# Side work of the SSD groups reordered in a hybrid GLA / Mamba-2 backbone: transposes on a second line, states in merged steps

## The chip, the core and the metric

The kernel runs on one core of a Trainium2 chip. Its engines are named as the profile names them: PE multiplies matrices (PEld loads its weights), DVE works on vectors, ACT evaluates functions and copies, POOL does further element-wise work, and SP issues the DMAs. Each engine executes its own instructions in the order in which the program lists them, and waits on semaphores where it needs another's result. The metric is the device time of one execution, in microseconds; a kernel is judged by the median of its runs.

## The reference

A backbone of two layers over 512 latent tokens and 256 context tokens, 1024 channels, all in float32. Layer 0 mixes tokens with chunked gated linear attention, layer 1 with a bidirectional Mamba-2 SSD; each mixer is followed by a squared-ReLU MLP of 4096 hidden channels, and every sub-layer is modulated and normalized. The change touches the SSD mixer alone. There a projection gives a gate z (2048 channels), x (2048), and for each of 8 groups a B and a C of 128 channels, and step sizes dt. x, B and C pass a centred convolution of five taps and a SiLU. A group has four heads of 64 channels. For each head and direction a state of 64 x 128 runs over the tokens:

```
cum = cumsum(dt * a)
decay = exp(cum[i] - cum[j]) for j <= i
y  = sum_j (C_i . B_j) * decay * dt_j * x_j   +   C_i . exp(cum_i) * s
s' = s * exp(last) + sum_j B_j * exp(last - cum_j) * dt_j * x_j
```

The context tokens are run first, forward and backward; their final states are the first states of the latent tokens. The output is (y_forward + y_backward + d * x) * SiLU(z), normalized, times an output matrix.

## The kernel before, in words

All large products are split: each float32 operand becomes a high and a low part (`wh`, `wl`, `xh`, `xl`), and a product is three matmuls (high-high, high-low, low-high; line 240). A weight tile of 128 x 1024 is loaded by SP into `raw` (four buffers), ACT casts the high part (L203), DVE subtracts for the low part (L204).

**Order.** The program lists the big projections in a row, and `worked` (line 179) counts their columns: each 768 columns are one step of a side clock. At each step the first generator of the list `side` may be advanced; it yields the number of steps that it wants to wait. So the work of group g, in `inner`, is dealt out between the projections of group g + 1. `drain` finishes a generator that is still there at a group's end. After that a scheduler lays down the order of each engine's instructions; it may move an instruction ahead where it believes the inputs ready.

**The SSD stage.** Tokens are in six chunks of 128: four latent (0 to 3), two of context (4, 5). For each of eight groups `group` projects and convolves B (`fB`), C (`fC`) and two tiles of x (`fx`), then projects two gate tiles (`gate_tiles`). A projection over both streams is 24 steps of the side clock, one over latent tokens alone 16, a group 120. A convolution (`conv`) is two ACT copies, one ACT and four DVE passes over 770 columns (L865, L867), then tanh and a last DVE pass, in two pieces for latent and context tokens (L869, L870).

Then `inner` does, in this order:

- `heads_rows`, `chunk_rows`: rows of cumulated decays are loaded from DRAM, broadcast to all partitions: `E` for whole heads, and per chunk two tiles `L`, one for each direction. There are seven `L` buffers. POOL masks each `L` (L912).
- `natural`: PE transposes `fB` and both `fx` chunk by chunk (L877); ACT copies the result to `Bn` and `xn` (L878; `xnat` in the profile).
- `prep`: DVE multiplies x of a chunk by its weights, in halves of 256 columns, one for each direction (L931, called by `scaled_by`). `dS`: PE multiplies by `Bn` (L943, L946).
- `chain`: one state step, a DVE product (L931) and a DVE sum (L951) of 256 columns. Eight of them, separately for the two directions, give the four states `ST` of each direction.
- the product of B and C of each chunk (`cb`, L963), copied to `cbs` by ACT (L965).
- `inter`: PE multiplies the states by `fC` (L986), DVE scales (L987, L989), POOL adds (L988).
- per chunk: `decays` (eight ACT exponentials of 128 columns, L998), `masks` (POOL adds both directions, L1001, which frees the second `L`; DVE multiplies by `cbs`, L1002), `outputs` (eight PE passes, L1009, and a DVE sum, L1012).
- the gated result `y` (L1031), its store, its square (ACT, L1036) and the sum of squares (POOL, L1037).

Small products share four PSUM banks (`sm`), the projections four others (`mm`). Behind the last group the output product starts with tiles loaded back and scaled (L1044, L1045).

## Time and profile before

| | |
|---|---|
| median of 3 runs | 1954.72 us (1950.36 to 1959.47) |
| profiled execution, span | 1959.6 us |
| PE busy | 1881.3 us (96%) |
| DVE, ACT, POOL busy | 1254.9, 798.6, 410.8 us |
| SSD groups | about 1015 to 1476 us of the span |
| one middle group | 60.5 us: PE 56.9, DVE 48.2, ACT 31.8, POOL 20.4 us |

The span is that of one execution, from the first to the last instruction; nothing of that execution is shown outside it. In the profile a row such as `PE sm L943 <- DVE xw L931: 14.6, 7, 3.6` says that PE, before writing a tile `sm` on line 943, waited for DVE's `xw` of line 931: 14.6 us in all, seven times, 3.6 us at most. A timeline row gives start, duration, engine, line, operation, out<-in, sizes, the number of instructions and, in brackets, the idle time before and who ended it. A matmul of float32 operands that are not split counts as two passes.

### The profile page before, as it was taken

Reading aid. Unit: us, or ns where it says so; the run is one execution under the profiler, and the core shown is the slowest. Engines: PE = TensorE matmul, PEld = TensorE weight load, DVE = VectorE, ACT = ScalarE, POOL = GpSimd, SP = SyncE. Lnnn points to the kernel's source line nnn. Section 1 sums busy time; section 2 is a strip of 40 time slices with the busy share of each in tenths; the row PEclk is TensorE's granted clock in tenths of the full one; section 3 lists DMA queues with packets and bytes.
Section 4 is the critical chain, followed back from the end, with each engine's and each line's share of the span. In section 5 each row is a group of like instructions: output and inputs, shape, how many; then the busy total and the mean of one; then the engine's idle time right before and its main releaser. Section 6 shows DMA issues by size and latency. Waiting matters only on the chain.

```text
span 1959.6 us, 29026 instructions
## 1 busy us (share of the span) xinstructions
PE 1881.3 (96%) x11405; PEld 1604.9 (82%) x11405; DVE 1254.9 (64%) x1929; ACT 798.6 (41%) x1386; POOL 410.8 (21%) x448
## 2 busy tenths in 40 slices
PE   7999999999999999999999999999999999999997
PEld 5988888788788888888897787777877788888886
DVE  4798887888655444324578888777887673333345
ACT  3445456454113123122366555455543353323231
POOL 2134242202002002010104432333321321102012
PEclk9999999999999999999999999999999999999999
DMA  8423313214444444313134433333434523333331
GB/s 329 156 73 114 104 36 106 65 55 150 141 142 140 138 137 135 116 41 116 33 107 121 129 115 112 104 101 129 121 100 132 164 73 105 96 99 96 96 89 54
DMA packets 78936, 219.01 MB, mean 112 GB/s; under 512 B 11056, under 2 KB 15792, under 8 KB 78800
## 3 DMA queue, kind: packets, MB, share of 16 engines
q1 hardware_dynamic: 78800, 217.17, 35.1%
q8 instruction: 89, 1.46, 0.3%
q14 instruction: 47, 0.39, 0.1%
HBM read 209.01 MB, written 8.13 MB: 111 GB/s over the span
## 4 chain that ended last, share of the span: by engine, by line
PE 63%; DVE 13%; DMA 7%; ACT 6%; POOL 5%; issue 5%; SPq 0%; DVEq 0%; POOLq 0%; ACTq 0%
PE mm L240 54%; DMA L<-crowc 4%; POOL L L1001 1%; ACT L L998 1%; DMA raw<-in_ada_wr_dram 1%; DVE A L593 1%; PE sm L943 1%; DVE raw L157 1%; DVE cv L867 1%; POOL L L912 1%; PE sm L676 1%; DVE wl L204 1%; POOL W L612 1%; PE sm L986 1%; PE mm L520 1%
## 5 line engine op out<-in xcount | busy, mean ns | idle before, releaser
L240 PE MATMUL mm<-xh,wh 128*128 128x512 f32 (+1 forms) x1824 | 554.2, 357 | 2.8 <-ACT xh L1044 2.6
L240 PE MATMUL mm<-xl,wh 128*128 128x512 f32 (+1 forms) x1824 | 550.0, 354 | 1.5 <-DVE xl L1045 1.5
L240 PE MATMUL mm<-xh,wl 128*128 128x512 f32 (+1 forms) x1824 | 549.7, 353 | 1.4 <-DVE wl L204 1.4
L203 ACT CAST wh<-raw 128x1024 fp32r<-128x1024 f32 (+3 forms) x227 | 227.8, 1004 | 658.5 <-PE mm L240 617.3
L204 DVE TENSOR_TENSOR wl<-raw,wh 128x1024 fp32r<-128x1024 f32 (+3 forms) x227 | 275.6, 1215 | 173.6 <-ACT wh L203 170.1
L240 PEld LDWEIGHTS mm<-xh,wh 128*128 128x128 f32 x1824 | 304.4, 189 | 54.4 <-ACT xh L1044 3.8
L240 PEld LDWEIGHTS mm<-xl,wh 128*128 128x128 f32 x1824 | 303.7, 189 | 50.6 <-issue 3.1
L240 PEld LDWEIGHTS mm<-xh,wl 128*128 128x128 f32 x1824 | 303.5, 189 | 50.7 <-DVE wl L204 2.5
L385 POOL TENSOR_TENSOR rq<-rr 128x768 f32<-128x768 f32 (+1 forms) x62 | 104.6, 1687 | 684.7 <-ACT rr L384 648.4
L240 PE MATMUL mm<-rl,wh 128*128 128x512 f32 x704 | 212.5, 355 | 3.8 <-DVE rl L387 3.8
L240 PE MATMUL mm<-rh,wl 128*128 128x512 f32 x704 | 212.4, 355 | 0.0
L240 PE MATMUL mm<-rh,wh 128*128 128x512 f32 x704 | 212.1, 355 | 0.0
L419 DVE SCALAR_TENSOR_TENSOR acc<-mm,row,acc 128x256 f32<-128x256 f32 (+1 forms) x182 | 100.7, 580 | 150.4 <-PE mm L240 150.0
L157 DVE SCALAR_TENSOR_TENSOR raw<-raw,srow 128x1024 f32<-128x1024 f32 x104 | 131.6, 1268 | 83.0 <-DMA raw<-in_ada_wr_dram 81.8
L867 DVE SCALAR_TENSOR_TENSOR cv<-pre,cvec,cv 128x770 f32<-128x770 f32 (+1 forms) x128 | 135.2, 1057 | 14.9 <-ACT cv L865 11.9
L240 PEld LDWEIGHTS mm<-rl,wh 128*128 128x128 f32 x704 | 116.0, 189 | 23.8 <-DVE rl L387 4.2
L240 PEld LDWEIGHTS mm<-rh,wh 128*128 128x128 f32 x704 | 116.1, 189 | 19.6
L240 PEld LDWEIGHTS mm<-rh,wl 128*128 128x128 f32 x704 | 116.1, 189 | 19.6
L998 ACT ACTIVATE L<-L,lcol 128x128 f32<-128x128 f32 x256 | 81.9, 393 | 69.1 <-POOL L L912 69.1
L387 DVE TENSOR_TENSOR rl<-rq,rh 128x768 fp32r<-128x768 f32 (+2 forms) x67 | 53.2, 794 | 64.0 <-POOL rq L385 63.7
L912 POOL TENSOR_SCALAR_AFFINE_SELECT L<-L 128x512 f32<-128x512 f32 x64 | 52.2, 817 | 142.5 <-DMA L<-crowc 141.4
L869 ACT ACTIVATE cf<-cv 128x512 f32<-128x512 f32 (+1 forms) x56 | 27.6, 533 | 86.5 <-DVE cv L867 86.5
(290 smaller groups left out, 2513.0 us busy)
## 6 DMA issues: line engine op xcount, KB each, us to landing
raw<-in_ffn_w_dram SPq DMA_DIRECT2D x112, 512.0 KB, 3.8
raw<-in_ada_wr_dram SPq DMA_DIRECT2D x80, 512.0 KB, 3.7
raw<-in_ssd_w_in_dram SPq DMA_DIRECT2D x48, 512.0 KB, 3.9
L<-crowc SPq DMA_DIRECT2D x64, 256.0 KB, 3.8
raw<-in_ada_w_dram SPq DMA_DIRECT2D x16, 512.0 KB, 9.1
raw<-in_gla_w_in_dram SPq DMA_DIRECT2D x16, 512.0 KB, 3.7
ec<-crow SPq DMA_DIRECT2D x64, 128.0 KB, 3.0
acc<-in_xT_dram SPq DMA_DIRECT2D x14, 384.0 KB, 6.9
```

The source lines that it names most:

```text
L157: nc.vector.scalar_tensor_tensor(o, raw, 1.0, srow[s], ALU.mult, ALU.mult, accum_out=t[:, b, s:s + 1])
L203: nc.scalar.copy(h, src)
L204: nc.vector.tensor_sub(l, src, h.bitcast(F32))
L240: nc.tensor.matmul(part_of(ps, t0, n), a[:, k, :], b[:, t0:t0 + n], start=(k == 0 and i == 0), stop=(k == kt - 1 and i == 2))
L385: eng.tensor_mul(q[:, a:b], r[:, a:b], r[:, a:b])
L387: nc.vector.tensor_sub(rl[:, a:b], q[:, a:b], rh[:, a:b].bitcast(F32))
L419: nc.vector.scalar_tensor_tensor(acc[m][:, t0:t0 + n], part_of(ps, t0, n), gate[:, m, s:s + 1], (src or acc)[m][:, t0:t0 + n], ALU.mult, A ...
L520: nc.tensor.matmul(ps[:, 256 * tt:256 * tt + 256], a, b, start=(k == 0 and i == 0), stop=(k == KT - 1 and i == 2))
L867: nc.vector.scalar_tensor_tensor(c[:, 0:n], pre[:, t:t + n], cw(t), c[:, 0:n], ALU.mult, ALU.add)
L869: nc.scalar.activation(f[:, t0:t1], c[:, t0 + d:t1 + d], AF.Tanh)
L912: nc.gpsimd.affine_select(out=L[z], in_=L[z], compare_op=ALU.is_ge, fill=NEG, base=0, pattern=[[0, 4], [1 - 2 * z, P]], channel_multiplier ...
L998: nc.scalar.activation(t[:, h, :], t[:, h, :], AF.Exp, bias=lcol[:, c, r:r + 1])
```

## The change

- **A second line of side work.** `worked` now advances two lists, `side` and `early`. A new generator `turned` is put on `early` as soon as both x tiles of a group are convolved, while its gate tiles are projected; it transposes B and the first x tile. The second x tile is transposed in `inner`, which stands on `side` as before. `Bn` and `xn` have two buffers each for that.
- **Context states summed in PSUM.** The weights `wc` of chunk 4 (forward) and 5 (backward) are multiplied once, in the set-up, by the decay over the other context chunk. The first state of both directions is then the sum of two products in one PSUM bank, which ACT copies.
- **Merged state chain.** The states are held as steps of both directions: `ST[i]` has the forward state of chunk i and the backward state of chunk 3 - i, with the decays of both in `dstep`. A step is a product and a sum of 512 columns; three steps make all states. `weighted` multiplies a chunk's x for both directions in one instruction; `ends` does chunks 0 and 3 in two halves.
- **Outputs in pairs.** Two chunks' products are written to one bank and added by one DVE sum of 512 columns.
- **Convolution.** Tanh and the last pass go over 770 columns at once; the context chunks are read two columns further on.
- `inner` yields other numbers, rows of chunk 0 and 1 are loaded at its start, chunks 2 and 3 after the second chunk's decays; `L` has eight buffers, `xt` four. The scratch that the program reserves for dynamic DMAs is set to 1024.

```diff
-LB = 7
-ZB = 2
-EB = 3
+LB = 8
+EB = 4
+NP = NT + 2
...
-    side, background = [], []
+    side, early, background = [], [], []
+    lanes = ((side, [0]), (early, [0]))
...
-            wait[0] -= 1
-            if wait[0] <= 0:
-                wait[0] = advance(side) or 1
+            for lane, wait in lanes:
+                wait[0] -= 1
+                if wait[0] <= 0:
+                    wait[0] = advance(lane) or 1
...
+            dtot = tt(sh, "dtot")
             nc.scalar.activation(dtot, po, AF.Exp)
+            for z, c in ((0, 4), (1, 5)):
+                zs = slice(32 * z, 32 * z + 32)
+                nc.vector.tensor_mul(wc[:, c, zs], wc[:, c, zs], dtot[:, 9 - c, zs])
+            nc.gpsimd.tensor_copy(dstep[:, :, 0, :], dtot[:, 0:3, 0:32])
+            for i in range(3):
+                nc.gpsimd.tensor_copy(dstep[:, i, 1, :], dtot[:, 3 - i, 32:64])
...
-            for t0, t1, d in ((0, 512, 0), (512, 768, 2)) if len(segs) > 1 else ((0, 512, 0),):
-                nc.scalar.activation(f[:, t0:t1], c[:, t0 + d:t1 + d], AF.Tanh)
-                nc.vector.scalar_tensor_tensor(f[:, t0:t1], f[:, t0:t1], 1.0, c[:, t0 + d:t1 + d], ALU.add, ALU.mult)
+            nc.scalar.activation(f[:, 0:n], c[:, 0:n], AF.Tanh)
+            nc.vector.scalar_tensor_tensor(f[:, 0:n], f[:, 0:n], 1.0, c[:, 0:n], ALU.add, ALU.mult)
...
             fx = [conv(2 * g + i, BOTH) for i in range(2)]
+            Bn = sp.tile([P, NCH, P], F32, tag="Bn", name=nm("Bn"), bufs=2)
+            xn = sp.tile([P, NCH, 256], F32, tag="xn", name=nm("xnat"), bufs=2)
+            early.append(turned(fB, fx, Bn, xn))
...
             drain()
-            side.append(inner(g, fB, fC, fx, zs))
+            drain(lane=early)
+            side.append(inner(g, fB, fC, fx, zs, Bn, xn))
+
+        def turned(fB, fx, Bn, xn):
+            yield 4
+            natural(fB, Bn)
+            yield 8
+            natural(fx[0], xn[:, :, 0:P])
+            yield 1
...
+            def weighted(c):
+                xw = sp.tile([P, 2, 256], F32, tag="xt", name=nm("xw"), bufs=EB)
+                w = wc[:, c, :].rearrange("p (z h) -> p z h", z=2)[:, :, heads]
+                x = xn[:, c, :].rearrange("p (h e) -> p h e", e=64).unsqueeze(1)
+                nc.vector.tensor_tensor(by_head(xw), x.to_broadcast(both), w.unsqueeze(3).to_broadcast(both), ALU.mult)
+                return xw
...
+            def step(i, d):
+                t = states()
+                w = dstep[:, i, :, heads].unsqueeze(3).to_broadcast(both)
+                nc.vector.tensor_tensor(by_head(t), by_head(ST[i]), w, ALU.mult)
+                nc.vector.tensor_add(t, t, d)
+                ST.append(t)
...
-            natural(fB, Bn)
-            yield 1
-            for i in range(2):
-                natural(fx[i], xn[:, :, i * P:(i + 1) * P])
-                yield 7
...
-            x4, x5 = prep((4, 4)), prep((5, 5))
-            yield 5
-            d4, d5 = dS(*x4), dS(*x5)
-            chain(ST[0][:, 0], d4[:, 0], 5, 0, d5[:, 0])
-            chain(ST[3][:, 1], d5[:, 1], 4, 1, d4[:, 1])
...
+            Rs, Ms = {0: chunk_rows(0), 1: chunk_rows(1)}, {}
+            x4, x5 = None, None
+            yield 2
+            natural(fx[1], xn[:, :, P:2 * P])
+            yield 2
+            x4, x5 = weighted(4), weighted(5)
+            xe = ends()
...
+            yield 8
+            x1 = weighted(1)
+            yield 3
+            d = sm_ps([P, 2, 256])
+            nc.tensor.matmul(d, Bn[:, 4, :], x4, start=True, stop=False)
+            nc.tensor.matmul(d, Bn[:, 5, :], x5, start=False, stop=True)
+            ST = [states()]
+            nc.scalar.copy(ST[0], d)
...
+            step(0, de)
+            yield 6
...
+            step(1, dd[0])
+            step(2, dd[1])
...
+            yield 4
+            decays(0)
+            yield 6
+            inter(0)
+            yield 5
+            inter(1)
+            yield 4
+            decays(1)
+            Rs[2] = chunk_rows(2)
+            Rs[3] = chunk_rows(3)
+            yield 14
+            outputs(0)
+            decays(2)
+            yield 14
+            decays(3)
+            yield 14
+            outputs(1)
+            yield 4
...
-    nc = _bacc.Bacc("TRN2", target_bir_lowering=False, num_devices=1)
+    nc = _bacc.Bacc("TRN2", target_bir_lowering=False, num_devices=1, dynamic_dma_scratch_size=1024)
```

The scheduler's order, not this text, decides what stands where. Ahead of the SSD stage and behind it the order of the kernel is the same. Three places in it, all at group 6; the numbers behind names are running ones, and differ between the two kernels.

ACT at the turn to the next group, before. `zs` are gate tiles, `Bn` and `xnat` the copies of transposes, `L` row tiles of the next group in their decays, `cbs` the copy of the product of B and C:

```order
L890 ACTIVATE zs_13147<-mm_13154 128x512
L203 CAST wh_13446<-raw_13444 128x1024
L878 COPY Bn_13211<-sm_13213 128x512
L878 COPY Bn_13211<-sm_13219 128x256
L878 COPY xnat_13212<-sm_13225 128x4x128
L878 COPY xnat_13212<-sm_13231 128x2x128
L998 ACTIVATE L_14084<-L_14084,lcol 128x128 x4
L878 COPY xnat_13212<-sm_13249 128x4x128
L878 COPY xnat_13212<-sm_13255 128x2x128
L998 ACTIVATE L_14136<-L_14136,lcol 128x128 x4
L965 COPY cbs_13309<-sm_13304 128x512
```

And now:

```order
L1014 ACTIVATE L_13742<-L_13742,lcol 128x128
L1014 ACTIVATE L_13929<-L_13929,lcol 128x128 x4
L203 CAST wh_13321<-raw_13319 128x1024
L898 ACTIVATE zs_13048<-mm_13055 128x512
L885 COPY xnat_12993<-sm_13126 128x4x128
L885 COPY xnat_12993<-sm_13132 128x2x128
L1014 ACTIVATE L_13930<-L_13930,lcol 128x128 x4
L974 COPY cbs_13152<-sm_13147 128x512
L1014 ACTIVATE L_13939<-L_13939,lcol 128x128 x4
L982 COPY ST_13181<-sm_13178 128x512
```

The copies of `Bn` and of the first x tile stand further ahead, out of these rows; the copies of the second x tile have one row tile's decays ahead of them, and behind them come two more, `L_13930` and `L_13939`, ahead of the copy of the first state.

POOL around the same place, now (`pre` are the margins of a convolution's input, `ssum` the sum of squares, AFFINE_SELECT the mask of a row tile, `TENSOR_TENSOR L` the sum of both directions, which frees the second tile's buffer):

```order
L1056 TENSOR_TENSOR ssum<-ssum,zs_12445 128x512
L1056 TENSOR_TENSOR ssum<-ssum,zs_12499 128x512
L926 AFFINE_SELECT L_13929<-L_13929 128x512
L862 MEMSET pre_13306 128x2
L863 MEMSET pre_13306 128x2
L1015 TENSOR_TENSOR L_13741<-L_13741,L_13742 128x512
L926 AFFINE_SELECT L_13930<-L_13930 128x512
L1015 TENSOR_TENSOR L_13929<-L_13929,L_13930 128x512
L926 AFFINE_SELECT L_13939<-L_13939 128x512
```

The buffer of `L_13742` goes to `L_13930`, and that of `L_13930` to `L_13939`, so each of these loads waits for the sum just above its mask; before, the same pairs of sum and mask stood there with the sums of squares between them.

DVE from the last gate tile on, now (`wl` a weight's low part, `xw` the weighted x, `L` the masked products, `ST` the states):

```order
L899 SCALAR_TENSOR_TENSOR zs_13048<-zs_13048,mm_13055 128x512
L940 TENSOR_TENSOR xw_13140<-xnat_12993,wc 128x512
L940 TENSOR_TENSOR xw_13142<-xnat_12993,wc 128x512
L948 TENSOR_TENSOR xw_13144<-xnat_12993,wc 128x256 x2
...
L1016 TENSOR_TENSOR L_13349<-L_13349,cbs_13152 128x512
L940 TENSOR_TENSOR xw_13183<-xnat_12993,wc 128x512
L957 TENSOR_TENSOR ST_13188<-ST_13181,dstep 128x512
L958 TENSOR_TENSOR ST_13188<-ST_13188,sm_13185 128x512
...
L957 TENSOR_TENSOR ST_13212<-ST_13209,dstep 128x512
L204 TENSOR_TENSOR wl_13443<-raw_13440,wh_13442 128x1024
L958 TENSOR_TENSOR ST_13212<-ST_13212,sm_13204 128x512
```

The masked products of all four chunks stand ahead of the first step; before, each stood behind some of the state steps, and the steps were sixteen instructions of 256 columns, those of the two directions in turn. A weight's low part stands between the product and the sum of the last step.

More of the change, by code (lines that the diff above doesn't have):

```diff
@@ L876, in natural @@
                 for c in range(c0, c1):
-                    nc.tensor.transpose(pt[:, c - c0, :], f[:, c * P:(c + 1) * P], ident)
+                    t0 = c * P + (2 if c >= NLC else 0)
+                    nc.tensor.transpose(pt[:, c - c0, :], f[:, t0:t0 + P], ident)
                 nc.scalar.copy(dst[:, c0:c1, :], pt[:, 0:c1 - c0, :])
@@ L913, in chunk_rows @@
                                             pattern=[[0, 4], [1 - 2 * z, P]], channel_multiplier=2 * z - 1)
-                    if z >= ZB:
-                        nc.gpsimd.tensor_add(L[z], L[z], hsl(lcol, c, z).unsqueeze(2).to_broadcast([P, 4, P]))
-                return L
-            Es = [heads_rows(i) for i in range(2)]
-            Bn = sp.tile([P, NCH, P], F32, tag="Bn", name=nm("Bn"), bufs=1)
-            xn = sp.tile([P, NCH, 256], F32, tag="xn", name=nm("xnat"), bufs=1)
-            natural(fB, Bn)
@@ L934, in prep @@
-            def prep(cs):
-                xw = sp.tile([P, 2, 256], F32, tag="xt", name=nm("xw"), bufs=EB)
-                for z, c in enumerate(cs):
-                    scaled_by(xw[:, z], xn[:, c], wc, c, z)
-                return xw, cs
-            def dS(xw, cs):
-                dp = sm_ps([P, 2, 256])
-                if cs[0] == cs[1]:
-                    nc.tensor.matmul(dp, Bn[:, cs[0], :], xw, start=True, stop=True)
-                else:
-                    for z, c in enumerate(cs):
-                        nc.tensor.matmul(dp[:, z], Bn[:, c, :], xw[:, z], start=True, stop=True)
-                return dp
@@ L949, in chain @@
-            def chain(dst, src, c, z, d):
-                scaled_by(dst, src, dtot, c, z)
-                nc.vector.tensor_add(dst, dst, d)
-            ST = [sp.tile([P, 2, 256], F32, tag="ST", name=nm("ST"), bufs=4) for _ in range(NLC)]
-            x4, x5 = prep((4, 4)), prep((5, 5))
-            yield 5
-            d4, d5 = dS(*x4), dS(*x5)
-            chain(ST[0][:, 0], d4[:, 0], 5, 0, d5[:, 0])
-            chain(ST[3][:, 1], d5[:, 1], 4, 1, d4[:, 1])
-            x03 = prep((0, 3))
+                return L
@@ new lines, in ends, with states @@
+            def ends():
+                xw = sp.tile([P, 2, 256], F32, tag="xt", name=nm("xw"), bufs=EB)
+                for z, c in enumerate((0, 3)):
+                    w = wc[:, c, 32 * z + 4 * g:32 * z + 4 * g + 4]
+                    x = xn[:, c, :].rearrange("p (h e) -> p h e", e=64)
+                    nc.vector.tensor_tensor(by_head(xw)[:, z], x, w.unsqueeze(2).to_broadcast(both[:1] + both[2:]), ALU.mult)
+                return xw
+            def states():
+                return sp.tile([P, 2, 256], F32, tag="ST", name=nm("ST"), bufs=4)
@@ L965, in inner @@
             nc.scalar.copy(cbs, cb)
[L966 to L976 removed]
+            yield 8
[6 more added lines that the diff above has]
+            nc.scalar.copy(ST[0], d)
+            x2 = weighted(2)
+            de = sm_ps([P, 2, 256])
+            for z, c in enumerate((0, 3)):
+                nc.tensor.matmul(de[:, z], Bn[:, c, :], xe[:, z], start=True, stop=True)
+            step(0, de)
+            yield 6
+            dd = [sm_ps([P, 2, 256]) for _ in range(2)]
+            for z, c, t in ((0, 1, x1), (1, 1, x1), (0, 2, x2), (1, 2, x2)):
+                nc.tensor.matmul(dd[(z + c + 1) % 2][:, z], Bn[:, c, :], t[:, z], start=True, stop=True)
+            step(1, dd[0])
+            step(2, dd[1])
             T = sp.tile([P, 2, NL], F32, tag="yn", name=nm("T"), bufs=1)
```

97 lines of the change are left out of this document (33 added, 64 removed).

## The prediction

> **What bounds the kernel now.** I read the page first, then the busy times by stretch, then TensorE's waits, then the timeline of one stall.
>
> ```profile
> span 1959.6 us, 29026 instructions
> PE 1881.3 (96%) x11405; PEld 1604.9 (82%) x11405; DVE 1254.9 (64%) x1929; ACT 798.6 (41%) x1386; POOL 410.8 (21%) x448
> ```
>
> TensorE is the bound, with 78 us idle. The next two rows set a stretch of the first FFN beside one period of the SSD stage (three columns of busy time with their counts: PE, PEld, DVE; then ACT, POOL; then the granted clock).
>
> ```profile
> 1343.00:1403.50 60.50, 56.94 (x317) 46.42 (x316) 48.18 (x73) 31.80 (x70) 20.38 (x27) 0.97 0.36 114
> 700.00:900.00 200.00, 200.00 (x1157) 174.83 (x1156) 76.47 (x102) 46.58 (x66) 22.06 (x13) 1.00 0.32 100
> ```
>
> In the FFN PE never stops: 1157 matmuls in 200 us are 0.346 us for a pair of 512 and 256 columns, which is one "turn" of 768 columns, the unit of the kernel's side clock. A group of the SSD stage has 120 turns, 41.5 us; the rest of its 60.5 us is side work on PE, 3.6 us of idle time and a lowered clock (0.97). DVE is busy 48 of 60 us and executes in order, so it is the engine that can become the next bound. Whom PE waits for, in groups 1 to 6 (1082 to 1448 us; first two rows), in group 0 (next three), and after group 7's projections (last):
>
> ```profile
> PE sm L943 <- DVE xw L931: 14.6, 7, 3.6
> PE sm L877 <- ACT Bn L878: 7.5, 4, 2.9
> ...
> PE sm L877 <- DVE cf L870: 3.3, 1, 3.3
> PE sm L943 <- DVE xw L931: 0.8, 2, 0.7
> PE sm L986 <- DVE ST L951: 0.4, 1, 0.4
> ...
> PE mm L240 <- ACT xh L1044: 2.6, 2, 2.3
> ```
>
> So 22.1 us in groups 1 to 6, at two places alone: the transposes, and the state products that follow them. How one of these stalls arises, in group 6:
>
> ```profile
> 1415.46 1.31 POOL L1001 TENSOR_TENSOR L<-L,L 128x512 f32<-128x512 f32 x1
> 1416.80 0.32 SPq L910 DMA_DIRECT2D L<-crowc  x1
> 1421.43 0.64 POOL L912 TENSOR_SCALAR_AFFINE_SELECT L<-L 128x512 f32<-128x512 f32 x1 [2.41 <-DMA L<-crowc]
> 1422.10 1.28 ACT L998 ACTIVATE L<-L,lcol 128x128 f32<-128x128 f32 x4 [4.28 <-POOL L L912]
> 1423.28 0.83 ACT L878 COPY xnat<-sm 128x512 f32<-128x512 f32 x2
> 1424.14 2.60 DVE L931 TENSOR_TENSOR xw<-xnat,wc 128x256 f32<-128x256 f32 x6 [6.29 <-ACT xnat L878]
> 1425.54 1.95 PE L943 MATMUL sm<-xw,Bn 128*128 128x512 f32 x4 [3.64 <-DVE xw L931]
> ```
>
> Read upwards: PE waits for `xw`, DVE for `xnat`, ACT's copy stands behind decays of the next group's rows, these wait for the select, it waits for a load, and the load was issued as soon as a POOL sum had freed a buffer (1416.77). **The stall is a late load, seen through ACT's order.** Its size depends on how much work lies between the transposes of the second x tile and the state products: 12 turns, 4.2 us.
>
> **What a stall costs besides itself.** The granted clock (third number from the end) behind three of these stalls, and behind the one of 3.64 us:
>
> ```profile
> 1180.63 3.12 PE L943 MATMUL sm<-xw,Bn 128*128 128x512 f32 x4 [2.11 <-DVE xw L931]
> 1181.30:1184.70 3.40, 3.40 (x9) 2.09 (x9) 2.53 (x8) 0.70 (x3) 0.64 (x1) 0.50 0.27 67
> 1242.70:1246.10 3.40, 3.40 (x8) 1.81 (x7) 2.40 (x8) 0.49 (x2) 0.63 (x1) 0.50 0.29 70
> 1365.60:1369.00 3.40, 3.40 (x13) 2.62 (x12) 3.04 (x9) 1.54 (x5) 0.63 (x1) 0.50 0.07 22
> 1425.00:1430.00 5.00, 4.46 (x21) 3.32 (x22) 5.00 (x15) 1.09 (x4) 0.63 (x1) 1.00 0.14 52
> ```
>
> A dip is 3.4 us at half clock, worth 1.7 us. One followed a stall of 2.11 us, none that of 3.64 us. Groups 1 to 6 have four (1181, 1243, 1297 and 1366 us): 6.8 us. The Trainium skill (TensorE: Matmul & The Clock Gate, Part 1) says that the clock halves after at least one idle window of about 3.4 us, the window running freely. By that rule two of the four at most would be the stalls' own, and the sum below would lose 3.4 us of gain (1934); the trace, with its dip behind 2.11 us, disagrees on the threshold.
>
> **The change, part by part.** The rows for the prices (DVE, then ACT, 1015 to 1475 us; mean ns behind the comma):
>
> ```profile
> L867 DVE SCALAR_TENSOR_TENSOR cv<-pre,cvec,cv 128x770 f32<-128x770 f32 x96 | 110.5, 1151 | 13.0 <-ACT cv L865 10.1 <-POOL L L1001 1.2
> L204 DVE TENSOR_TENSOR wl<-raw,wh 128x1024 fp32r<-128x1024 f32 x46 | 62.5, 1358 | 12.4 <-ACT wh L203 12.2
> L931 DVE TENSOR_TENSOR xw<-xnat,wc 128x256 f32<-128x256 f32 x70 | 29.8, 472 | 29.8 <-ACT xnat L878 29.8
> L870 DVE SCALAR_TENSOR_TENSOR cf<-cf,cv 128x512 f32<-128x512 f32 x32 | 22.5, 703 | 8.3 <-ACT cf L869 8.3
> L951 DVE TENSOR_TENSOR ST<-ST,sm 128x256 f32<-128x256 f32 x56 | 22.0, 410 | 3.6 <-PE sm L946 2.0 <-PE sm L943 1.5
> L870 DVE SCALAR_TENSOR_TENSOR cf<-cf,cv 128x256 f32<-128x256 f32 x24 | 20.9, 872 | 0.0
> L1002 DVE TENSOR_TENSOR L<-L,cbs 128x512 f32<-128x512 f32 x28 | 18.9, 679 | 0.0
> L1012 DVE TENSOR_TENSOR T<-T,sm 128x256 f32<-128x256 f32 x28 | 11.5, 410 | 0.0
> L857 ACT COPY pre<-mm 128x512 f32<-128x512 f32 x32 | 18.5, 577 | 0.0
> ```
>
> And from the timeline a row load with its select, a block of outputs (PE), the tanh of the second x tile with the first transposes behind it, the cb product (L963) and a pair of half-wide state products (L946; the wide pair is above, 1.95):
>
> ```profile
> 1363.59 0.33 SPq L910 DMA_DIRECT2D L<-crowc  x1
> ...
> 1366.79 0.63 POOL L912 TENSOR_SCALAR_AFFINE_SELECT L<-L 128x512 f32<-128x512 f32 x1 [3.23 <-DMA L<-crowc]
> ...
> 1388.52 0.66 PE L1009 MATMUL sm<-L,xnat 128*64 128x128 f32 x8
> 1409.63 0.94 ACT L869 ACTIVATE cf<-cv 128x512 f32<-128x512 f32 x2 [1.17 <-DVE cv L867]
> 1412.78 0.82 PE L877 MATMUL sm<-ident,cf 128*128 128x128 f32 x6
> 1427.34 1.05 PE L963 MATMUL sm<-cf,cf 128*128 128x128 f32 x8
> 1428.58 1.03 PE L946 MATMUL sm<-xw,Bn 128*128 128x256 f32 x4
> ```
>
> - *DVE's load.* Weighted x: ten halves at 0.47 were 4.7 us; now four of 512 at 0.68 and two halves, 3.7. State chains: eight products and eight sums, 7.1; now three of each at 0.68, 4.1. The convolution's last step: 0.70 + 0.87 becomes one of 770, at most the 1.15 of L867, three times: 1.3 less. Outputs: four at 0.41 become two at 0.68: 0.3 less. Together **5.6 us less per group**, about what the period can shrink by, so DVE stays as full as it was. The four products of the once-only set-up add under 2 us, beside other work.
> - *PE's work.* Columns stay the same. Two output blocks fewer per group save an entry and an exit each; I take 2 us in all, between 0 and 4 (a block of eight passes takes 0.66 us, most of it not its own columns).
> - *Transposes.* Those of the B tile and of the first x tile now stand in the gate projections, 28 and 21 turns ahead of where they were, and their copies no longer queue with the second x tile's. Between that tile's transposes and the state products lie 2 turns, the cb product and 11 turns: 0.7 + 1.0 + 3.8 = 5.5 us, of which copies and two weighted products need 0.6 + 0.8 + 1.4 = 2.8. The slack grows from under 1 us to about 2.7. Both stalls of groups 1 to 6 go: **-22.1 us, and the dips, -6.8 us**.
> - *What is late next.* The first state is now an ACT copy (L982), and ACT's order puts it behind decays of two row tiles of the next group. These loads run one behind the other, since each takes the buffer that the sum of the pair before frees. I count from the second x tile's transposes (t = 0). Above, the tanh of that tile ends at 1410.57, and the first transposes, one turn behind the gate projections, start at 1412.78: 1.9 us from the tanh to the projections' end. The transposes now stand 2.7 turns behind it, so the tanh ends at -2.8 and the last decay behind it at -2.4. Then POOL sum 1.3, load 3.2 to 4.6 (3.2: issue at 1363.59, select at 1366.79; 4.6: above), select 0.64, decays 1.28, POOL sum 1.3, load, select, decays, copy 0.58: the copy ends at 11.0 to 13.8. Then three products and three sums of 0.68 and one weight split of 1.36 that stands among them: 5.4, so the last state is there at 16.4 to 19.2. PE gets to the products that read it at 0.6 + 5.5 + 1.8 (two state products) + 1.0 + 2.1 (6 turns) + 1.8 + 3.5 (10 turns), and 0.7 into the block: 17.0. **New stall: 0 to 2.2 us a group; I take 1.0** (about the middle), six times: +6 us. Group 7 loads no rows after itself.
> - *Group 0.* Its convolutions are late on DVE because ACT waits for the row loads of the set-up; that remains. The first x tile's transposes come 36 turns (12.6 us) after the B tile's and want the result some 2.7 us before it is there (before: 3.3); the second x tile, the state products and the first steps, which now follow each other on PE without projection matmuls between, add some 3 us. Against 4.5 before: +1.5, between -4.5 and +5.
> - *Behind group 7.* The scaling for the first output block now stands ahead of the last gate's tanh on ACT: of 2.9 us, 2 go.
> - *Loads, eight row buffers for seven, wider convolution tiles, smaller DMA scratch:* no instruction is added on SP; all of it lies beside PE. I take 0; eight buffers let loads start earlier, which the chain above already has.
>
> Sum: -22.1 - 6.8 + 6 + 1.5 - 2 - 2 = -25.4 us. The profiled execution spans 1959.6, about the highest run shown (1959.5; the median is 1954.7), so the sum gives 1934 from its span and 1929 from the median. If the runs differ by the number of dips, part of the gain is missing in the median run. **I predict 1931 us.**
>
> **The rivals.**
>
> *The stall moves and keeps most of its size (1950 us).* With loads at 4.6 us the new wait is 2.2 us a group, and every second one is followed by a dip, as 2.11 was: 6 x 2.2 + 3 x 1.7 = 18. With 1 us more at the second x tile's transposes, whose input DVE finishes only 1 us or so ahead (tanh at -2.8, then a weight split and the last product), 24 in place of 6. That is 1931 + 18, some 1950. For it: ACT already lost the most here by waiting for POOL, and DVE has no more spare time than before. Against: loads that nothing else ran beside took 3.2.
>
> *Nothing changes (1953 us).* The copies of the second x tile still stand right behind one row tile's decays on ACT. If these are late by the 4.28 us of the row above, 1.6 us of stall at the old place, and the new one, would remain: 6 x (1.6 + 2.2) = 23, with two dips 26 in place of 6: 1931 + 20, and 2 for the outputs' saving if that is 0. Against: that row tile's load is now issued before the `y` stores, not behind them.
>
> The next row is SP's wait for a row buffer that a POOL sum frees, the second that load's median time to land.
>
> ```profile
> SPq L910 <- POOL L L1001: 104.8, 31, 6.3
> ...
> L<-crowc SPq DMA_DIRECT2D x64, 256.0 KB, 3.8
> ```
>
> *Slower (1971 us).* One mechanism, the two loads in series ahead of the first state. The state's copy delays DVE's steps, these the weight split behind them, this the raw weights' load that stands ahead of the row loads in SP's order, and so the next row loads: it feeds itself. Break-even is a new loss of 4.8 us a group (28.9 / 6): a stall of 3.1 with its dip, the copy at 14.7. With loads of 6.5 us each it ends at 17.6, a stall of 6.0 and a dip each: 6 x 7.7 = 46, 40 more than I took: 1971. SP's waits speak for it, the median load of 3.8 us against it.
>
> **How the numbers follow.** Forecast 0.63 (own range 1919 to 1942: new stall 0 to 2 us, group 0 either way); all of the SSD stage's idle time gone (1917 and below) 0.05; stall moved 0.16; nothing 0.10; slower 0.06. Low end: 1931 less 6 (new stall), 6 (group 0) and 2 (blocks) is 1917. High end: the first rival's 1950. Range 1917 to 1950. A difference under 0.5% (1945 to 1964 is "same") is about what a measurement of this kernel can tell from no change. Faster: 0.63 + 0.05 + about two thirds of the moved stalls, 0.11; same: the rest of these and the second rival, 0.14; slower 0.07.
>
> **What would show it.** Right: no PE wait over 1 us at the transposes or state products of groups 1 to 6, periods of 55 to 57 us, clock dips in at most one or two groups, and what is left as waits of the state-to-output products for `ST`, with ACT's copy of the first state behind decays that wait for POOL. Wrong: PE still waiting for `xw` or the transposes' inputs, DVE idle for `xnat` as long as now (29.8 us), or a period over 58 us. If the `ST` wait is absent and the time is under 1920, my chain of loads is too slow; if it is 4 us or more a group, the third rival holds.

## The result: 0.6% slower, 37 us above the forecast

| | before | after |
|---|---|---|
| median, us (20 runs each) | 1957.31 | 1968.26 |
| span of the profiled execution, us | 1959.6 | 1970.1 |
| its PE idle time, us (span less PE busy) | 78.3 | 87.2 |

The ratio is 1.0058, with a 95% interval of 1.0040 to 1.0075: clearly not faster, and slower by about the half per cent up to which the prediction speaks of "same". Forecast were 1931 us in a range of 1917 to 1950, and slower had a chance of 0.07.

The head of the page of the changed kernel, which answers to the first fence of the prediction:

```profile
span 1970.1 us, 28913 instructions
PE 1882.9 (96%) x11437; PEld 1617.9 (82%) x11437; DVE 1253.1 (64%) x1779; ACT 800.2 (41%) x1370; POOL 417.7 (21%) x452
```

DVE executes 150 instructions fewer and is busy as long as before (1254.9). Five group periods, from the product of B and C in group 1 to that in group 6 (busy time and count of PE, PEld, DVE, ACT, POOL; then the granted clock), before:

```profile
1122.30:1427.30 305.00, 287.07 (x1591) 232.76 (x1590) 241.34 (x366) 161.70 (x345) 102.38 (x135) 0.98 0.36 113
```

and after:

```profile
1122.10:1432.10 310.00, 285.34 (x1612) 241.49 (x1612) 244.83 (x273) 163.44 (x336) 107.16 (x135) 0.96 0.36 112
```

The period went from 61.0 to 62.0 us; 55 to 57 was forecast. PE's waits in groups 1 to 6 of the changed kernel:

```profile
PE sm L884 <- DVE cf L876: 27.4, 6, 5.5
PE sm L1003 <- DVE ST L958: 2.5, 3, 1.3
```

Both old places are empty. (Of the 2.5 us in the second row, 1.3 still belong to group 0.) In their stead stands one stall of 3.5 to 5.5 us in each group, at the transposes of the second x tile, which wait for the last step of its convolution. At every one the clock halves, for 3.4 or 6.8 us; in the two longer dips it does so while PE still waits. The six stretches, in the columns of above:

```profile
1119.90:1123.30 3.40, 3.40 (x17) 3.21 (x16) 2.26 (x3) 2.34 (x5) 0.81 (x1) 0.51 0.65 199
1181.40:1188.20 6.80, 5.35 (x21) 5.01 (x22) 6.13 (x8) 3.83 (x10) 1.81 (x3) 0.50 0.61 195
1242.80:1249.60 6.80, 4.60 (x19) 4.41 (x20) 6.43 (x9) 3.83 (x10) 2.47 (x2) 0.50 0.61 193
1307.70:1311.10 3.40, 3.40 (x16) 3.21 (x15) 3.33 (x6) 1.08 (x3) 0.64 (x1) 0.50 0.84 249
1369.10:1372.50 3.40, 3.40 (x16) 3.21 (x15) 3.40 (x7) 0.86 (x2) 0.76 (x1) 0.50 0.76 252
1430.50:1433.90 3.40, 3.40 (x17) 3.21 (x15) 3.40 (x7) 0.86 (x2) 0.00 (x0) 0.51 0.72 217
```

Over all six that is 27.2 us at half clock in groups 1 to 6, in 23.6 of which PE is busy; before it was 13.6. Over the whole of these two executions the times at half clock are equal (30.7 us), because the one of before has dips outside these groups that the other lacks, and the mean granted clock of both is 0.990. Over all runs it is lower now: its median is 0.987 in 20 runs, against 0.991 in 75 runs of the kernel before.

How one stall arises, in group 5: the timeline of ACT, DVE and POOL ahead of the transposes at 1368.52 (the second x tile's projection ends about 1350.8, the gates' at about 1364.15, when the transposes could start).

```profile
1348.60 0.32 SPq L924 DMA_DIRECT2D L<-crowc  x1
...
1351.54 0.85 ACT L875 ACTIVATE cf<-cv 128x770 f32<-128x770 f32 x1 [3.22 <-DVE cv L874]
1352.37 0.64 POOL L926 TENSOR_SCALAR_AFFINE_SELECT L<-L 128x512 f32<-128x512 f32 x1 [3.80 <-DMA L<-crowc]
1353.04 1.28 ACT L1014 ACTIVATE L<-L,lcol 128x128 f32<-128x128 f32 x4 [0.65 <-POOL L L926]
1354.23 1.04 ACT L203 CAST wh<-raw 128x1024 fp32r<-128x1024 f32 x1
1355.17 1.14 ACT L1055 ACTIVATE zs<-y 128x512 f32<-128x512 f32 x2
1356.22 0.56 ACT L864 COPY pre<-mm 128x512 f32<-128x512 f32 x1
...
1357.43 1.03 ACT L872 ACTIVATE cv<-pre,cvec 128x770 f32<-128x770 f32 x1
1358.56 6.22 DVE L874 SCALAR_TENSOR_TENSOR cv<-pre,cvec,cv 128x770 f32<-128x770 f32 x4 [1.31 <-ACT cv L872]
...
1364.70 0.68 DVE L899 SCALAR_TENSOR_TENSOR zs<-zs,mm 128x512 f32<-128x512 f32 x1
1365.30 1.22 DVE L204 TENSOR_TENSOR wl<-raw,wh 128x1024 fp32r<-128x1024 f32 x1
1366.43 2.03 DVE L876 SCALAR_TENSOR_TENSOR cf<-cf,cv 128x770 f32<-128x770 f32 x1
...
1368.52 0.33 PE L884 MATMUL sm<-ident,cf 128*128 128x128 f32 x1 [4.37 <-DVE cf L876]
```

ACT fetches the finished projection 5.4 us late (1356.22). Ahead of it stand the tanh of the first x tile, late by DVE, then four decays with a wait of 0.65 us for their row load (1.9 us together), a weight cast and two squares. These decays are not due yet: counted in the program's order, eight loads a group, the load at 1348.60 is the 50th of 64, which is chunk 0 of group 6, while the gates of group 5 are still being projected. The first product that reads this chunk starts at 1460.0, 107 us later. Then DVE's four taps take 6.22 us in place of 4.1 (four of the median 1.02), and a gate product and a weight split come ahead of the last step.

Which DVE operations grew: groups by shape, 1015 to 1488 us (mean ns behind the comma).

```profile
L874 DVE SCALAR_TENSOR_TENSOR cv<-pre,cvec,cv 128x770 f32<-128x770 f32 x96 | 120.7, 1257 | 26.3 <-ACT cv L872 20.9 <-POOL ssum L1056 1.8 <-POOL L L926 0.9
L876 DVE SCALAR_TENSOR_TENSOR cf<-cf,cv 128x770 f32<-128x770 f32 x24 | 31.1, 1295 | 6.3 <-ACT cf L875 6.3
L1016 DVE TENSOR_TENSOR L<-L,cbs 128x512 f32<-128x512 f32 x28 | 22.9, 868 | 6.7 <-ACT cbs L974 6.7
L957 DVE TENSOR_TENSOR ST<-ST,dstep 128x512 f32<-128x512 f32 x21 | 15.1, 718 | 15.9 <-ACT ST L982 15.4
L1005 DVE TENSOR_TENSOR T<-sm,ec 128x512 f32<-128x512 f32 x14 | 9.6, 684 | 0.0
```

A tap went from 1151 to 1257 ns, a mask (L1016) from 679 to 868; their counts and sizes are the same.

### The profile page after: what moved, and what is told of

The parts are those of the page before. It is cut to its first block, busy times and chain, and to the rows that moved or that the text cites. A ratio compares the mean times of both kernels' runs of the same rounds, so it can differ in the third digit from the quotient of the medians.

```text
span 1970.1 us, 28913 instructions
## 1 busy us (share of the span) xinstructions
PE 1882.9 (96%) x11437; PEld 1617.9 (82%) x11437; DVE 1253.1 (64%) x1779; ACT 800.2 (41%) x1370; POOL 417.7 (21%) x452
## 4 chain that ended last, share of the span: by engine, by line
PE 59%; DVE 16%; DMA 7%; POOL 6%; ACT 6%; issue 5%; SPq 1%; DVEq 0%; POOLq 0%; ACTq 0%
PE mm L240 51%; DMA L<-crowc 5%; DVE cv L874 3%; POOL L L1015 1%; PE sm L676 1%; POOL T L1006 1%; DMA raw<-in_ada_wr_dram 1%; DVE A L593 1%; POOL L L926 1%; DVE wl L204 1%; ACT L L1014 1%; DVE raw L155 1%; POOL W L612 1%; PE mm L520 1%; DMA raw<-in_ada_w_dram 1%
## 5 line engine op out<-in xcount | busy, mean ns | idle before, releaser
L874 DVE SCALAR_TENSOR_TENSOR cv<-pre,cvec,cv 128x770 f32<-128x770 f32 (+1 forms) x128 | 145.0, 1133 | 28.0 <-ACT cv L872 21.9
L926 POOL TENSOR_SCALAR_AFFINE_SELECT L<-L 128x512 f32<-128x512 f32 x64 | 61.0, 958 | 126.0 <-DMA L<-crowc 126.0
L875 ACT ACTIVATE cf<-cv 128x770 f32<-128x770 f32 (+1 forms) x32 | 25.4, 793 | 92.9 <-DVE cv L874 92.9
```

The costliest lines, as they stand in the source:

```text
L874: nc.vector.scalar_tensor_tensor(c[:, 0:n], pre[:, t:t + n], cw(t), c[:, 0:n], ALU.mult, ALU.add)
L875: nc.scalar.activation(f[:, 0:n], c[:, 0:n], AF.Tanh)
L926: nc.gpsimd.affine_select(out=L[z], in_=L[z], compare_op=ALU.is_ge, fill=NEG, base=0, pattern=[[0, 4], [1 - 2 * z, P]], channel_multiplier ...
```

## The experiments

Three theories stood at the start. **The place:** the transposes were put too near to the end of the convolution. **Row loads:** ACT stands still for decays that wait for loads. **DVE is full:** its work sets the period. "Period" below is a fifth of the time from the first product of B and C in group 1 to that in group 6, taken from the trace (61.0 before, 62.0 after); ratios are against the kernel before, on the same chip, with their 95% interval. Runs of different chips are compared by their ratios.

### Single edits

**The transposes 12 turns later** (e1).

```
-            yield 2
+            yield 14
             natural(fx[1], xn[:, :, P:2 * P])
```

> The changed kernel with the second x tile's transposes 14 turns behind the gate projections in place of 2 (all that follows in the side work 12 turns, 4.2 us, later). Theory 'the place' (the transposes stand before the convolution's last step on DVE, cf L876, which is late by 3.5 to 5.5 us against TensorE): the six stalls shrink to 0 to 1.3 us each, the six half-clock dips go, some 35 us in all: about 1933 us (1928 to 1942). Theory 'row loads' (cf is late because ACT's first step of that convolution stands behind decays that wait for row loads) says the same here, since the delay is 4.4 us wherever it comes from. Theory 'DVE is full' (its busy time stayed at 1253 us, so it sets the period of 61.5 us): the wait only moves to the state products; period stays at 60 us or more, 1955 to 1968 us.

1971.5 us, ratio 1.0083 (1.0051 to 1.0116), period 63.2. PE's waits and, behind them, DVE's:

```profile
PE sm L991 <- DVE xw L940: 19.3, 6, 4.1
PE sm L979 <- DVE xw L940: 10.4, 6, 2.3
```

```profile
DVE xw L940 <- ACT xnat L885: 28.3, 6, 5.2
```

The transposes wait no more, but 29.7 us stand at the state products: the copies of `xnat` are late on ACT, where decays wait 64.8 us for selects. So the place alone is not the cause.

**Ten row buffers** (e2; `LB = 10`).

> The changed kernel with ten row buffers in place of eight; TensorE's order is the same. 'Row loads': a pair of loads no longer waits for the sum of the pair before it, so some 4 us (the landing time, median 4.2) leave the chain ahead of ACT's first step of the second x tile's convolution; the stalls of 3.5 to 5.5 us fall below 1.5 and the dips go: 1930 to 1942 us. 'The place' and 'DVE is full': no change, 1960 to 1972 us.

1975.5 us, 1.0080 (1.0050 to 1.0109), period 63.0; the same stall, 29.9 us in six. Two buffers more do not help.

**Without the second line** (e3; all three transposes behind the gates, at turns 1, 2 and 9).

```
-            early.append(turned(fB, fx, Bn, xn))
...
-            yield 2
+            yield 1
+            natural(fB, Bn)
+            yield 1
+            natural(fx[0], xn[:, :, 0:P])
+            yield 7
             natural(fx[1], xn[:, :, P:2 * P])
```

> The changed kernel without the second line of side work: transposes of the B tile, the first and the second x tile behind the gate projections, at 1, 2 and 9 turns as before; merged chain, summed context states and paired outputs stay. 'The place': the convolution is done by turn 9 (3.2 us later than now), so the stall is 0 to 2 us and 13 turns lie between transposes and state products: 1930 to 1945 us, faster than before, that is, the second line alone lost the gain. 'Row loads' and 'DVE is full': the merged chain and what it does to ACT's and DVE's order lost it: a stall remains at the transposes or at the state products, 1950 to 1970 us.

1979.3 us, 1.0119 (1.0081 to 1.0157), period 62.0: the rest of the change alone is slower too, and slower than either theory said; PE waits 22.6 us at the transposes, for the copies of `Bn`.

**The second line alone** (e4; the edit of the diff on the kernel before, second x tile at turn 2).

> The kernel before with the second line of side work alone (transposes of B and the first x tile in the gate projections, those of the second x tile 2 turns behind them, two buffers for their outputs, smaller DMA scratch to make room); chains, state products and outputs as before. 'The place': stalls of 3 to 6 us at the second x tile's transposes waiting for the convolution, six dips: 1960 to 1978 us, no better than before. 'Row loads' (as a result of the merged chain's order): the transposes wait less than 1.5 us, and the gain of up to 25 us shows: 1930 to 1945 us.

1962.5 us, 1.0028 (1.0004 to 1.0052), period 59.9. PE waits 15.7 us for the convolutions' last step, in 12 waits, where it waited 22.1 at two other places. This part is about neutral. The time lies in the range that 'the place' gave, with shorter stalls than it gave.

**Without row loads** (e5).

```
-                    nc.sync.dma_start(L[z]..., crowc[z, c, g:g + 1]...)
-                    nc.gpsimd.affine_select(out=L[z], in_=L[z], ...
+                    nc.gpsimd.affine_select(out=L[z], in_=rowz[:, z], ...
```

> The changed kernel with the row loads left out: POOL's select reads one constant tile, so the decays come out as zero and the within-chunk products are left out of the result; all instructions but these 64 loads stay. The first three runs moved PE's stall about and left the period at 61 to 63 us, so something beside PE sets it. Theory 'waits for loads': the loads of 3 to 5 us, one behind the other, of which two to four stand on the side chain of each group, set the period: without them it falls to 56 to 58 us, 1925 to 1945 us in all. Theory 'DVE's work': DVE is busy some 49 of 61.5 us and waits 11, of which the loads cause the smaller part (waits for ACT's state copy and masks, 3.8 a group): the period falls by 0 to 3 us, 1948 to 1968 us.

1962.1 us, 1.0008 (0.9983 to 1.0033), period 61.6: by the ratios some 10 of the 37 us that were missing. That is less than 'waits for loads' gave (1945 us or below); the granted clock is 0.94 from 1122 to 1430 us, lower than the 0.96 of the changed kernel. The place of the stall is unchanged:

```profile
PE sm L886 <- DVE cf L878: 22.1, 6, 4.2
```

**One tap less** (e6; `for t in (0, 1, 3)`).

> The changed kernel with the convolution's last tap (t = 4) left out: four DVE operations a group less, 3 x 1.24 + 0.73 = 4.4 us of DVE's work, all else stays. 'DVE's work': the period falls by 4 us or more (to the 57 us that PE needs), the stalls at the transposes go, and the time falls by 30 to 45 us: 1923 to 1940 us. 'Waits for loads': DVE then waits longer for the same loads; 0 to 2 us a group, 1952 to 1968 us.

1969.0 us, 1.0054 (1.0029 to 1.0079), period 62.5, though DVE's work fell by some 5 us a group. The stall went to the state products, as in e1, and for the same reason (PE's first wait, DVE's, then ACT's):

```profile
PE sm L979 <- DVE xw L940: 19.8, 6, 3.7
```

```profile
DVE xw L940 <- ACT xnat L885: 28.0, 6, 5.1
```

```profile
ACT L L1014 <- POOL L L926: 78.1, 24, 6.1
```

**Tanh in two passes** (e7) and **side work spread** (e8; 18 turns in place of 14, three times).

> The changed kernel with the last step of the convolutions in two passes again (512 and 256 columns, tanh and product each). If one pass of 770 is what makes the second x tile late (tanh and product follow each other whole: 0.85 + 1.0 to 2.0 us in series), the stalls shrink by some 0.5 to 1 us each: 1955 to 1965 us. If DVE's work sets the period: same to 3 us slower, 1966 to 1975 us.

> The changed kernel with 18 turns in place of 14 between the pairs of products, so that a group's side work ends at turn 98 in place of 86 (before: 104). If DVE is short of time only because the change packed its side work into the four convolutions and left the gate projections free of it, some of the 4 to 5 us stalls go: 1940 to 1958 us. If the whole of DVE's work or the waits in series set the period: no change, 1963 to 1973 us.

e7: 1978.4 us, 1.0092 (1.0056 to 1.0129). e8: 1985.7 us, 1.0140 (1.0106 to 1.0174), period 65.0, with 17.6 us of waits for `ST`. Neither is the cause. Single edits all leave the period at 60 to 65 us (and one below, at 66), and e1, e2, e3, e6, e7 and e8 all came out slower than any of their theories said.

### Two at a time

Each edit uncovered another wait of about the same size. So a fourth theory: **several chains of nearly equal length** stand beside PE (DVE's work with the convolution; decays on ACT waiting for rows), and only what takes away two of them is seen.

> The changed kernel without the row loads and without the last convolution tap (both leave work out, as in the two runs before). Theory 'several chains of nearly equal length': each of the two alone only uncovered the next chain (without the loads the convolution's last step was still 3.5 to 4.2 us late, with a tap less the weighted x was, behind decays that waited for loads); together both waits go: stalls under 1.5 us, few dips, period 55 to 57 us, 1922 to 1940 us. Theory 'something else holds the period at 61 us' (neither loads nor DVE's work; PE's side work itself, or the half clock): 1955 to 1970 us.

> The changed kernel without the row loads and with the second x tile's transposes at turn 14. 'Several chains': the convolution's step that was 3.5 to 4.2 us late without loads gets 4.2 us more, and the copies and weighted x behind it no longer queue behind waiting decays: stalls under 1.5 us each, 1922 to 1942 us. 'Something else': 1955 to 1970 us.

> The changed kernel with one tap less and the transposes at turn 14, row loads as they are. 'Several chains', with the loads as the one that stays: the stalls at the weighted x (2.3 to 3.7 us with one tap less, 1.5 to 4.1 with the transposes at 14) remain, 1955 to 1970 us. If the loads matter little and DVE's work with the place is the whole: 1925 to 1945 us.

No loads and one tap less: 1934.3 us, 0.9903 (0.9876 to 0.9930), period 57.5. The five periods and PE's waits:

```profile
1116.80:1404.10 287.30, 276.85 (x1612) 232.58 (x1611) 216.92 (x250) 163.19 (x335) 100.52 (x136) 1.00 0.26 83
```

```profile
PE sm L886 <- DVE cf L878: 10.7, 6, 2.1
PE sm L979 <- DVE xw L940: 1.7, 6, 0.3
```

By the ratios, the two alone gained some 10 us and 1 us against the changed kernel; together 30, and no stretch at half clock is left in these periods. No loads and turn 14 gave 1947.4 us, 0.9964 (0.9945 to 0.9983), a gain of some 18 us, between the ranges of the two theories. One tap less and turn 14, with the loads, gave 1965.2 us, 1.0050 (1.0029 to 1.0070): 21.8 us still stand at the state products (3.6 a group). The loads are in every pair that gains.

**Row loads from GpSimd** (e12; `nc.gpsimd.dma_start` for L924).

> The changed kernel with its row loads issued by GpSimd in place of the sync engine; the result is the whole computation. On the sync engine they stand behind loads of raw weights that wait for a weight split on DVE (141.8 us of waits in groups 1 to 6, the longest 11.0) and behind the decay rows ec. If that order is what makes them late, the rows come 2 to 5 us earlier and the stalls shrink: 1935 to 1955 us. If their own latency of some 4 us after the sum that frees the buffer is what counts, or GpSimd's issue costs as much: 1960 to 1980 us.

1997.5 us, 1.0215 (1.0189 to 1.0241), the slowest of all; POOL is busy 448.1 us in place of 417.7, and a load still lands 4.0 us after its issue (4.2 in the changed kernel). Taking the loads out of SP's order gains nothing this way.

### The order on ACT

The row loads could count by their latency, or because the order of ACT puts decays that nobody needs yet ahead of work that PE needs soon. The next edit leaves the loads as they are and ties each decay behind the convolution that was listed last before it:

```
-            nc.scalar.activation(c[:, 0:n], pre[:, 2:2 + n], AF.Identity, ...)
+            mark[0] = nc.scalar.activation(c[:, 0:n], pre[:, 2:2 + n], AF.Identity, ...).ins
...
-                        nc.scalar.activation(t[:, h, :], t[:, h, :], AF.Exp, ...)
+                        with tc.issue_after(mark[0]):
+                            nc.scalar.activation(t[:, h, :], t[:, h, :], AF.Exp, ...)
```

> The changed kernel, whole, with one constraint on the order: each decay (ACT, L1014 in the changed kernel) is issued behind the first ACT step of the last convolution listed ahead of it, so that no decay of the next group stands ahead of the convolutions. Row loads stay as they are. If it is ACT's order that makes the loads count, this is worth as much as leaving the loads out (1962 us there) or more, since ACT has less to do ahead of the second x tile: 1935 to 1962 us. If the loads count by their latency alone (decays then come late for the masks and the products): 1965 to 1980 us.

1971.8 us, 1.0068 (1.0043 to 1.0093), period 63.2: no gain, and in the range of 'latency'. ACT's decays wait for row selects no more in groups 1 to 6 (60.1 us in the changed kernel), and the transposes do not wait; but the first products now come before their masks:

```profile
PE sm L1028 <- DVE L L1019: 31.0, 11, 5.4
```

**The same, and the side work 12 turns later** (e14, `yield 14`), **and the sum `T` on DVE** (e15, L1006 from `nc.gpsimd` to `nc.vector`).

> The same order with the second x tile's transposes at turn 14. ACT's order as cause: like the run without loads and with turn 14 (1947 us) or better, 1930 to 1950 us, with all of the computation. Latency as cause: 1963 to 1975 us, as with turn 14 alone (1971).

> As the run before, and the sum T (L1006) on DVE in place of POOL: 14 sums of 0.6 us more on DVE, 14 waits of 1.2 us of DVE for POOL less, and 2 us of POOL beside which DVE's passes over SBUF run up to 1.8 times as long. Expected 0 to 8 us below the run before; if DVE's work is now the bound alone, up to 5 us above it.

e14: 1948.4 us, 0.9950 (0.9924 to 0.9977), period 58.7. Later side work gained nothing alone (e1); here it gains 23. e15: 1937.7 us, 0.9896 (0.9863 to 0.9929), period 57.0, all of the computation done. Its five periods, and PE's waits in groups 1 to 6 (lines shifted by the edit: the products with the states, and those with the masks):

```profile
1117.50:1402.60 285.10, 277.72 (x1613) 232.72 (x1612) 239.36 (x280) 162.35 (x336) 81.69 (x125) 1.00 0.40 120
```

```profile
PE sm L1005 <- DVE ST L960: 5.1, 7, 0.8
PE sm L1028 <- DVE L L1019: 4.1, 5, 1.2
```

So the loads' latency is not what holds the kernel at 1968 us: with the same loads, in another order, the gain is there. Again it takes two edits: the order alone (e13) and the later side work alone (e1) gain nothing.

### Is it the change, or the order?

**The kernel before with the order** (e16), **and with all three edits** (e17: decays behind the convolution, all side work 13 turns later by a `yield 13` ahead of the first transposes, the sum on DVE).

> The kernel before with the same constraint on the decays. Its 22 us of stalls in groups 1 to 6 arise from copies of xnat behind decays that wait for a late row load. ACT's order as cause: they go and their dips, about 1957 less 22 to 29: 1926 to 1940 us, and the change itself would then be worth nothing. If the stall has another cause behind it (the convolution's last step), it only moves: 1950 to 1965 us.

> The kernel before with decays behind the convolution, all side work 12 turns later and the sum T (L988) on DVE. If the three edits are the whole gain and the change adds nothing: as fast as the changed kernel with them, 1934 to 1942 us. If the change's fewer, wider operations are worth what the prediction gave for DVE (5.6 us less a group): 15 us or more above that, 1950 us or more. From the rows after, the change saves DVE some 2 to 3 us a group in states, weighted x and outputs, once its passes no longer run beside POOL: I expect 1940 to 1950 us.

e16: 1952.4 us, 0.9963 (0.9941 to 0.9986), period 59.8; its 22 us of stalls went, and 14.7 came at the products, where the profile names no releaser, each of the six with a dip of 3.4 us: the stall mostly moved, as the second branch said. e17: 1942.3 us, 0.9911 (0.9876 to 0.9947), period 56.3:

```profile
1125.20:1406.60 281.40, 279.50 (x1591) 228.99 (x1590) 241.03 (x376) 163.68 (x345) 89.30 (x125) 1.00 0.39 122
```

PE is idle 1.9 us in five periods, less than in e15 (7.4). Between the two totals, 1942.3 and 1937.7, the intervals overlap. Most of the gain comes from the three edits; what the change itself adds to them cannot be told from nothing, and its periods are longer (57.0 against 56.3).

**Group 7's decays last** (e18: e15, with `mark[0]` set to the tanh of the last gate tile in group 7).

> The changed kernel with the three edits, and group 7's decays behind the tanh of its last gate tile on ACT. The stalls of 3.0 and 2.2 us behind group 7 and their dip of 6.8 us at half clock (3.4 us) lie behind decays of 3.1 and 1.0 us on ACT and the scaled tiles after them: 3 to 8 us less, 1930 to 1935 us. If the scaled tiles wait for their rows of y instead: no change, 1936 to 1940 us.

1934.7 us, 0.9884 (0.9851 to 0.9918). The time lies in the first branch's range, but cannot be told apart from e15, and the stalls behind group 7 stayed (2.4 and 2.3 us, in e15 3.0 and 2.2): no gain is shown. It is the fastest kernel that computes everything.

| | median us | ratio | period us |
|---|---|---|---|
| the change | 1968.3 | 1.0058 | 62.0 |
| no loads / one tap less / both | 1962.1 / 1969.0 / 1934.3 | 1.0008 / 1.0054 / 0.9903 | 61.6 / 62.5 / 57.5 |
| order / order, later / and sum | 1971.8 / 1948.4 / 1937.7 | 1.0068 / 0.9950 / 0.9896 | 63.2 / 58.7 / 57.0 |
| before: order / three edits | 1952.4 / 1942.3 | 0.9963 / 0.9911 | 59.8 / 56.3 |

## Why the prediction was wrong

**Transposes: the step that failed.** "Both stalls of groups 1 to 6 go: -22.1 us, and the dips, -6.8 us." They went from their places, but 27.4 us stand at the second x tile's transposes, and the half clock doubled. The term is +5.3 for the waits and, as an estimate, +5.3 for the clock (PE is busy for 23.6 us at half clock, before for 13.0; half of the difference): +10.6 in place of -28.9. That is 39 us, as much as the whole gap of 37. The slack was worked out for the state products (2.7 us), and not for the transposes ahead of them. There the timeline of before gave it: the tanh 1.9 us ahead of the projections' end, and a weight split and a product still to come. The text named this ("only 1 us or so ahead") in a rival, and priced it at 1 us more a group; it measured 4.6.

The reason behind it is general. The times of DVE and ACT were kept where the old trace had them, while PE was moved ahead by some 5 us a group. In the order that they had, these engines seem to have had no 5 us to give. That is inferred: with PE's old stalls gone the period was still 59.9 (e4), and other single edits left it at 59.8 to 65.6. It was the order more than the amount of work: e17 does the work of the kernel before, one sum moved from POOL to DVE, with the same DVE time (241.03 us against 241.34), in a period of 56.3. PE's stall was the visible end of chains beside it.

**DVE's load: wrong.** "5.6 us less per group" measured +0.7 (244.83 less 241.34, over five). Two parts. The removed pieces were short ones that overlap their neighbours: the busy time counts an overlap once, while the prediction added up durations. Six weighted halves at 472 ns each took 2.60 us together, not 2.83. Over the five periods the durations of all DVE instructions add up to 264.5 us before and 256.1 after, and the overlap falls from 23.1 to 11.3. And what stayed got slower: taps by 0.106 us (twelve a group, 1.3 us) and masks by 0.19 (four, 0.8 us). They now run beside POOL for longer: the 96 taps of 770 columns for 49.7 us in all, before 37.4, while the taps that overlap nothing of POOL take 1.01 to 1.02 us in both kernels. The last step of the convolution, taken at 1.15 at most, measured 1.295. e6 shows that 5 us less would not have helped alone.

**What is late next: right mechanism, small size.** The state's copy does stand behind decays, and DVE waits 15.4 us for it (L957 above); PE waits 1.2 us for `ST` in groups 1 to 6, where 6 were taken. PE comes late itself by then, which is the likely reason; no run separates it. **Group 0** (+1.5): its waits are 7.8 us now against 4.5, +3.3, in the range. **Behind group 7** (-2): 3.2 us of waits against 2.9, no gain. **Output blocks** (-2): not seen in this pair. With the clock at 1.00 in both, PE is busy 277.72 us in five periods of e15 and 279.50 in those of e17, 1.8 less: about the size of the term, though the two kernels differ in more than the blocks.

**The rivals.** "The stall moves" (0.16) named this place beside another, and gave 1950 us by a price too small. "Slower" (1971 us, 0.06) is near the measured time by luck: its mechanism is another, the loads in series ahead of the first state. Rows that ACT waits for did matter (e5, e9, e14, e15), but through the copies and convolutions behind them in ACT's order, not through the state.

**What would show it** held: a PE wait at the transposes' inputs, and a period over 58 us. DVE's idle time for `xnat`, 29.8 us before, is gone from the changed kernel, and waits for ACT's state copy, convolution steps and weight casts took its place.

**What stays open:** why the second line alone (period 59.9 against 61.0) does not gain in the total. Its trace shows where the gain goes, not why: the first product of B and C in group 0 comes 2.0 us later, and from that of group 6 to that of group 7 it takes 63.2 us in place of 59.0. Open is also which of the change's other parts makes its period longer by 2 us, and how the gain of e15 divides among its three edits.

## What to carry to other kernels

A stall of the bounding engine can be the visible end of a longer chain beside it. Before pricing its removal, move that engine ahead by the gain hoped for and ask of every input whether its in-order producers can be that much earlier too; if one cannot, the stall only moves. When single edits all give nothing, try two together before the theory is dropped: here 1 and 10 us made 30. And look in an engine's order for work that is not yet due and waits for a transfer ahead of work that is; tying it behind is cheap.

## What the runs showed of the hardware

**Passes of DVE over SBUF slow down beside POOL.** The four taps of the stall above in the chain of waits of the changed kernel, and POOL in the same time:

```profile
1358.56 1.89 DVE cv L874
...
1360.47 1.96 DVE cv L874
...
1362.52 1.22 DVE cv L874
...
1363.76 1.03 DVE cv L874
```

```profile
1358.33 3.27 POOL L1056 TENSOR_TENSOR ssum<-ssum,zs 128x512 f32<-128x512 f32 x2
1361.56 1.36 POOL L926 TENSOR_SCALAR_AFFINE_SELECT L<-L 128x512 f32<-128x512 f32 x1
```

Beside POOL these taps take up to 1.96 us, free of it 1.03. In the changed kernel 46 of the 96 taps of 770 columns overlap no instruction of POOL and take 1.01 to 1.02 us each; the others take 1.01 to 2.05, so not every overlap costs. Products with one input in PSUM (L1005) keep their 684 ns, beside POOL too (681 and 687). The Trainium skill (SBUF — State Buffer, Who interferes with whom) says that a DVE instruction with two SBUF inputs contends with a GpSimd instruction that reads SBUF, and that one with at most one such input, outside the two-port modes, does not. The rows agree, and the prediction would have needed it for DVE's load.

**The clock.** In the changed kernel all six stalls of 3.5 to 5.5 us came with 3.4 or 6.8 us at half clock; in e9, waits of 1.6 to 2.1 us at the same place were followed by none in groups 1 to 6, though one of 2.11 had been before. In e16, six waits of 2.3 to 2.5 us had a dip of 3.4 us each. The length of a wait alone does not tell in these runs whether a dip follows.
